# Column norms of the squared weights: adding the row tiles on GpSimd ahead of one product with ones

## The chip, the cores and the metric

The kernel runs on one core of a Trainium2 chip. The metric is the device time of one execution in microseconds (us), the median of several. A core has TensorE (PE in the profile, with PEld for the loading of weights into the array), VectorE (DVE), ScalarE (ACT), GpSimd (POOL) and SyncE (SP, which here only issues DMAs). Each engine works off its own queue in order and waits on semaphores; an instruction that has to wait holds up all that is queued behind it on that engine.

## The reference, cut to what matters

One layer of a hybrid encoder over 4096 tokens of width 1024:

```
h = rmsnorm(x, pre_norm_g)
q, k, v, g_a, u_p, g_p = split(h @ w_in)            # widths 512, 128, 128, 512, 512, 512
a = banded_attention(q, k, v, rel_bias, sink) * silu(g_a)
p = multiscale_pool(u_p, pool_w, pool_scale) * silu(g_p)
x = x + rmsnorm(concat([a, p]) @ w_out, post_norm_g)
```

multiscale_pool takes a centred mean over windows of 2, 4, 8 and 16 tokens minus the token in each of four channel groups, and then a 128x128 linear map per group (pool_w).

The sums of squares that this change is about do not stand in the reference. The kernel multiplies in pairs of float16 numbers that together carry a float32, and for that it scales each weight matrix by a power of two, taken from the largest sum of squares over a column.

## The kernel before

There are two stages. The first, the part up to about 448 us of the profile, projects x onto the gates and the pooled branch (g_p, u_p, g_a), does the pooling, and prepares all weights. The second does q, k, v, the attention and the output. Only the first is touched.

**Weights.** A weight tile is 128 columns of w_in, held as 128 partitions by 1024 numbers: eight row tiles of 128x128 side by side. The pooled gate g_p, the attention gate g_a (GA in the code) and the pooled branch (UU) have four such tiles each; k, v and q have six in all. For UU the tile is first made on TensorE, as the product of a piece of w_in with pool_w (u_prod), and evicted twice by ScalarE, once squared (u_square), once as it is (u_keep).

**Norms.** `norms` runs over the tiles of a group: ScalarE squares a tile into one of two bf16 buffers (w_square, buffer sqt), and `w_norm` forms on TensorE the product of a 128x128 matrix of ones with each of the eight row tiles, added up in one PSUM tile. So every partition holds the sums of squares of the 128 columns. When all tiles of the group are in, `w_scale` on VectorE takes the largest and makes the power of two (lines 582 to 585). From it ScalarE (w_high) and VectorE (w_low) write the float16 pair that the products of the projection read. The groups are "ga" and "gb" (two tiles each, both of the pooled gate, in spite of the name), "a4" (the four tiles of GA), "u4" (the four of UU, from the loop at line 954), and "b1" (the one value tile, in wb_steps). The profile calls their PSUM tiles n2ga, n2gb, n2a, n2u and n2b. The other tiles of w_b and w_out have only a total formed (total_square) and use the same two buffers.

**Order.** The first stage's order is worked out by a planner, the class Steps. Every step is booked with its engine, a length in us, a key (its due time), what it reads and what it writes. `run` goes through the booked time: an engine that comes free takes the ready step with the lowest key, and a step is ready 0.2 us (GAP) after the last one that it depends on has ended. Then all steps are issued in the order of their booked starts. That order is fixed in the queues; a step that takes longer on the chip than booked makes the queue wait, not change. A squaring is booked with 0.2 + 1024 x 0.00088 = 1.1 us, w_norm with 0.5.

**Around the change.** While a4 is done, TensorE works on `plain` for the pooled gate (products "plain" in the profile, L689), VectorE on the operands of x (b_low, narrow subtractions into xb) and on sums of weights for later row blocks (sum_weights, wide additions into wq, then into raw), through the helper `tt` (L307). GpSimd's work in this stage is the root of the row norms (`root`, lines 323 and 324) and later the gate of the pooling (`pool_gate`, line 885). The products of GA follow those of the pooled gate, and those of UU follow them.

Of the kernel before, what the change touches and what calls it, by code (L numbers as in the profile page):

```python
# [8 lines left out]
F32 = mybir.dt.float32  # L9
# [4 lines left out]
ALU = mybir.AluOpType  # L14
# [3 lines left out]
P = 128  # L18
# [116 lines left out]
def hybrid_layer(ctx: ExitStack, tc, io, out):  # L135
    nc = tc.nc
# [12 lines left out]
    ones16 = const.tile([P, P], BF16, name="ones16")  # L149
# [36 lines left out]
    def scale_pow(dst, n2, floor, top):  # L186

        m2 = comm.tile([P, 1], F32, name="m2", tag="m2")
        nc.vector.tensor_reduce(out=m2, in_=n2, axis=mybir.AxisListType.XY, op=ALU.max)
        scale_of(dst, m2, floor, top)  # L190
# [20 lines left out]
    with ExitStack() as actx:  # L211
        pa = actx.enter_context(tc.tile_pool(name="pa", bufs=1))
        psa = actx.enter_context(tc.tile_pool(name="psa", bufs=1, space=PSUM))
# [14 lines left out]
        sqt = [pa.tile([P, D], BF16, name=f"sq{i}") for i in range(2)]  # L228
# [6 lines left out]
        def turn(name):  # L235
            turns[name] += 1
            return turns[name] % 2
# [44 lines left out]
        do = st.add  # L282
# [4 lines left out]
        def act(n):  # L287
            return 0.2 + n * 0.00088
# [5 lines left out]
        def ld(key, dst, src, mb, r=(), w=()):  # L294
            do("SP", 0.45, key, nc.sync.dma_start, dst, src, r=r, w=w, dma=mb / 0.3)

        def t_scalar(eng, out, in0, s1, op0, s2=None, op1=None):
            if op1 is None:
                eng.tensor_scalar(out=out, in0=in0, scalar1=s1, scalar2=None, op0=op0)
            else:  # L300
                eng.tensor_scalar(out=out, in0=in0, scalar1=s1, scalar2=s2, op0=op0, op1=op1)

        V, G, A = nc.vector, nc.gpsimd, nc.scalar


        def tt(eng, out, in0, in1, op):
            eng.tensor_tensor(out=out, in0=in0, in1=in1, op=op)  # L307
# [211 lines left out]
        for c in range(HK):  # L519
            do("ACT", act(512), -5 + 0.1 * c, first_square, c,  # L520
               r=[f"n0.{c}.0"], w=[f"xsq{c}"])
# [10 lines left out]
        for u in range(2):  # L532
# [3 lines left out]
            for c in range(HK):  # L536
                do("DVE", 0.85, k + 0.5 * c, norm_half, c, u,
                   r=["gs"] + [f"bc{i}" for i in (2 * u, 2 * u + 1)],
                   w=[f"n0.{c}.{u}"])
                do("ACT", act(512), k + 0.5 * c + 0.1, b_high, 0, c, u, r=[f"n0.{c}.{u}"],  # L540
                   w=[f"xb0.{c}.{u}h"])
                e, us = ("POOL", 1.4) if c in LOW0[u] else ("DVE", dve(512))
                do(e, us, k + 0.5 * c + 0.2, b_low, 0, c, u,
                   r=[f"n0.{c}.{u}", f"xb0.{c}.{u}h"], w=[f"xb0.{c}.{u}l"])
# [20 lines left out]
        n2_t = {}  # L565
# [7 lines left out]
        def w_norm(z, group, i, n, b):  # L573
            if i == 0:
                n2_t[group] = psa.tile([P, n, P], F32, name=f"n2{group}", tag=f"n2{b}")
            for k in range(KT):
# [2 lines left out]
                    stop=(k == KT - 1), skip_group_check=True,  # L579
                )  # L580

        def w_scale(group, cols):
            scale_pow(sw[:, cols], n2_t.pop(group), 1e-20, W_SCALE)
            t_scalar(V, sc[:, cols], sw[:, cols], gh, ALU.mult)
            V.reciprocal(isc[:, cols], sc[:, cols])
# [4 lines left out]
        def norms(keys, last, views, reads, group, cols):  # L590
            n, b = len(views), turn("n2")
            for i, (key, view, r) in enumerate(zip(keys, views, reads)):
                z = turn("sq")
                do("ACT", act(D), key, w_square, view, z, r=r, w=[f"sqt{z}"])
                do("PE", 0.5, key + 0.5, w_norm, z, group, i, n, b,
                   r=["ones", f"sqt{z}"] + ["summed"] * (group == "ga"), w=[f"n2{b}"])
            do("DVE", 1.5, last, w_scale, group, cols, r=["gs"], w=[f"n2{b}", f"sw{group}"])

        def tile_view(q, i):
# [26 lines left out]
        def sum_weights(q, scale, group, key, step, eng, again=False):  # L626
# [8 lines left out]
            if again:  # L635
# [11 lines left out]
            pair(q, S4, 1, scale, key + 3.5 * step, group)  # L647

        norms([5, 5], 5, [tile_view(GP, i) for i in (0, 1)], [tile_keys(GP, i) for i in (0, 1)],
              "ga", slice(0, 2))  # L650
        do("PE", 1.4, 6, turn_over, 24, r=["ones", "swga"], w=["bankv"])
        do("PE", 0.9, 5.6, row_prod, r=["row", "yt0", "summed"], w=["n20"])
        do("ACT", 0.7, 5.6, row_keep, w=["n20", "yt0"])
        for i, op, key in ((0, A11, 9.5), (1, A12, 12.5)):
            pair(GP, op, i, sw[:, 0:1], key, "ga")
        norms([13, 13], 13, [tile_view(GP, i) for i in (2, 3)], [tile_keys(GP, i) + ["w4h"] * (i == 3) for i in (2, 3)],
              "gb", slice(2, 4))

# [255 lines left out]
        for u in range(2):  # L914
            do("SP", 0.45, 60 + u, lambda u=u: nc.sync.dma_start(x_scr[u], xb[0][:, u]),
               r=[f"xb0.{c}.{h}{v}" for c in range(HK) for h in range(2) for v in "hl"], dma=3.5)


        norms(range(24, 28), 28, [tile_view(GA, i) for i in range(4)],
              [tile_keys(GA, i) for i in range(4)], "a4", slice(4, 8))  # L920

# [31 lines left out]
        U0 = 36.0  # L953
        b = turn("n2")
        for j in range(4):
            ld(9.5 + 0.1 * j, wut[:, j], io["w_uT"][j], 0.5, w=[f"wut{j}"])
            z = turn("sq")
            for half in range(2):
                t = U0 + 4 * j + 2 * half
                do("PE", 1.0, t, u_prod, j, half, r=["ws", f"wut{j}"], w=[f"wup{half}"] + bcs)  # L960
                do("ACT", act(512), t + 1.2, u_square, j, half, z, r=[f"wup{half}"], w=[f"sqt{z}"])
                do("ACT", act(512), t + 1.2, u_keep, j, half, r=[f"wup{half}"],
                   w=[f"tile{UU}.{j}{half}"])
            do("PE", 0.5, U0 + 4 * j + 5, w_norm, z, "u4", j, 4, b, r=["ones", f"sqt{z}"],
               w=[f"n2{b}"])
        for j in range(4):
            do("DVE", 0.01, U0, lambda: None, r=[f"tile{UU}.{j}{half}" for half in range(2)],
               w=[f"tile{UU}.{j}"])
        do("DVE", 1.5, U0 + 18, w_scale, "u4", slice(8, 12), r=["gs"], w=[f"n2{b}", "swu4", "u4"])

        plain_weights(UU, (sw[:, 8:9],) * 2, ("u4",) * 2, (52, 54, 60, 62))
# [868 lines left out]
    V, G = nc.vector, nc.gpsimd  # L1840
# [24 lines left out]
    z = 0.0  # L1865
# [149 lines left out]
    z = now[0]  # L2015
# [177 lines left out]
```

## Time and profile before

| | us |
|---|---|
| time, median of 3 runs | 1161.74 (1161.5 to 1162.57) |
| profiled execution, its own time | 1162.76 |
| profiled execution, span from first to last instruction | 1161.0 |
| VectorE busy in the span | 947.8 (82%) |
| GpSimd busy in the span | 313.7 (27%) |
| mean granted TensorE clock | 0.996 |

How to read it: a row of the timeline gives the start in us, the duration in us, the engine, the line of the kernel, the operation, what it writes and reads, the shape and how many alike were merged; in square brackets stands how long the engine had been idle and who ended that. A row of the table by stretch gives the stretch, its length, and then the busy time and the instructions of PE, PEld, DVE, ACT and POOL, the granted TensorE clock, the share of the DMA engines and GB/s. A row by tile gives the shortest, middle and longest duration in ns, and the first and the last start. Products are pipelined: a record is longer than the time for which it holds the array, and the distance from start to start is what counts.

### The profile page before, as it was taken

What the parts mean: (1) busy time and instruction counts of PE and PEld (TensorE: products, weight loads), DVE (VectorE), ACT (ScalarE), POOL (GpSimd) and SP (SyncE); (2) the same over time, 40 slices, a digit from 0 to 9 for tenths busy, and PEclk for the clock granted to TensorE, in tenths of its full rate; (3) what the DMA queues carried; (4) which work ended last, traced back from release to release, by engine and by line L of the source; (5) the groups of instructions that cost most, each with busy time, mean ns of one, the idle gap of its engine ahead of it and who ended that gap; (6) DMA issues with size and microseconds to landing.
All of it is one profiled execution on the core that took longest, in us unless ns stands there. A gap on an engine that the chain in (4) does not pass through costs nothing. (4 is left out here: it accounts for less than half of the span.)

```text
span 1161.0 us, 32325 instructions
## 1 busy us (share of the span) xinstructions
PE 1146.3 (99%) x13420; PEld 873.5 (75%) x13420; DVE 947.8 (82%) x1875; ACT 717.7 (62%) x1485; POOL 313.7 (27%) x310
## 2 busy tenths in 40 slices
PE   8999999999999999999999999999999999999997
PEld 7998888888888888886667676576666767667653
DVE  6889988988799974568878888878887888887886
ACT  6876556536654542257676776676667677667772
POOL 0001120211111010201524433532533443353231
PEclk8999999999999999999999999999999999999999
DMA  9645575867667664299975886788777688777885
GB/s 344 217 128 180 174 259 183 285 229 238 227 190 225 206 179 134 76 289 242 250 185 144 197 211 143 200 202 177 177 196 184 148 198 215 140 196 165 178 216 143
DMA packets 301683, 228.36 MB, mean 197 GB/s; under 512 B 219568, under 2 KB 259504, under 8 KB 296928
## 3 DMA queue, kind: packets, MB, share of 16 engines
q1 hardware_dynamic: 301536, 226.30, 72.5%
q8 instruction: 105, 1.72, 0.6%
q14 instruction: 42, 0.34, 0.1%
HBM read 114.68 MB, written 60.34 MB: 151 GB/s over the span
## 5 line engine op out<-in xcount | busy, mean ns | idle before, releaser
L689 PEld LDWEIGHTS <-wq 128*128 128x128 f16 x4104 | 401.6, 98 | 50.4 <-DVE wq L310 2.6
L689 PE MATMUL y<-xt,wq 128*128 128x256 f16 x1512 | 203.3, 273 | 0.1
L1347 ACT ACTIVATE p<-p,nm 128x385 f32<-128x385 f32 (+1 forms) x256 | 152.9, 599 | 36.5 <-POOL p L1330 20.3
L1273 PE MATMUL aq<-xb,xb 128*128 128x256 f16 x1024 | 173.4, 273 | 0.2 <-DVE mo L1715 0.2
L1273 PEld LDWEIGHTS <-xb 128*128 128x128 f16 x1536 | 150.1, 98 | 26.4 <-issue 8.0
L1676 PE MATMUL ms<-wo,ys 128*128 128x512 f16 x720 | 163.7, 379 | 0.0
L1377 DVE SCALAR_TENSOR_TENSOR pn<-p,rd,pn 128x384 f16<-128x384 f32 (+1 forms) x256 | 157.6, 667 | 5.9 <-ACT pn L1369 5.9
L1336 DVE CUSTOM_DVE_ANT_0 p<-s,nt,nsink 128x384 f32<-128x384 f32 (+1 forms) x256 | 156.0, 666 | 2.0 <-PE s L1313 2.0
L1273 PE MATMUL aq<-xb,xt 128*128 128x256 f16 x512 | 139.6, 273 | 0.4 <-issue 0.4
L1369 ACT ACTIVATE pn<-p,rd 128x384 f16<-128x384 f32 (+1 forms) x256 | 134.8, 596 | 4.4 <-issue 1.1
L307 POOL TENSOR_TENSOR yt<-yt,sg 128x512 f32<-128x512 f32 (+2 forms) x32 | 51.0, 1594 | 301.6 <-DVE yt L310 214.8
L1676 PEld LDWEIGHTS <-ys 128*128 128x128 f16 x720 | 68.1, 98 | 83.9 <-POOL ys L1582 4.8
L1676 PE MATMUL m<-wo,y 128*128 128x512 f16 x540 | 121.8, 379 | 0.0
L1676 PEld LDWEIGHTS <-y 128*128 128x128 f16 x540 | 51.4, 98 | 63.5 <-ACT at L1543 2.9
L1273 PE MATMUL kv<-xb,xb 128*128 128x256 f16 x512 | 86.7, 273 | 0.0
L1710 POOL TENSOR_TENSOR mo<-mo,gpost 128x512 f32<-128x512 f32 x39 | 63.7, 1634 | 84.4 <-ACT jkb L1699 83.2
L1273 PEld LDWEIGHTS <-xt 128*128 128x128 f16 x768 | 75.1, 98 | 10.6 <-issue 0.8
L689 PE MATMUL plain<-xb,wq 128*128 128x256 f16 x576 | 68.0, 276 | 2.1 <-DVE wq L310 2.0
L1273 PE MATMUL kv<-xb,xt 128*128 128x256 f16 x256 | 69.8, 273 | 0.0
L689 PE MATMUL v<-xt,wq 128*128 128x256 f16 x504 | 68.6, 273 | 0.1
L689 PE MATMUL v<-xb,wq 128*128 128x256 f16 x504 | 68.6, 273 | 0.0
L689 PE MATMUL y<-xb,wq 128*128 128x256 f16 x504 | 68.6, 273 | 0.0
(221 smaller groups left out, 1854.3 us busy)
## 6 DMA issues: line engine op xcount, KB each, us to landing
nt<-in_xT SPq DMA_DIRECT2D x28, 512.0 KB
x_scr<-xb SPq DMA_DIRECT2D x14, 1024.0 KB
xb<-x_scr SPq DMA_DIRECT2D x14, 1024.0 KB
xr<-in_x SPq DMA_DIRECT2D x28, 512.0 KB
out<-xr SPq DMA_DIRECT2D x28, 512.0 KB
xn<-in_x SPq DMA_DIRECT2D x27, 512.0 KB
ga_scr<-cc SPq DMA_DIRECT2D x64, 128.0 KB
raw<-in_w_out SPq DMA_DIRECT2D x16, 512.0 KB
```

The lines of the kernel that those rows point to most:

```text
L307: eng.tensor_tensor(out=out, in0=in0, in1=in1, op=op)
L689: nc.tensor.matmul(b[:, s], wq[:, slot[q, op], wv, s, k, :], x[:, xv, k, :], start=(first and k + s + wv + xv == 0), stop=(last and k == H ...
L1273: nc.tensor.matmul(acc, w[:, j, k, :], x[:, kh, v, kt, :], start=(n == 0), stop=(n == 3 * KT - 1),)
L1336: nc.vector.tensor_tensor_reduce(out=p_t[b, half][:, hh, :nk], in0=s_t[jj][:, gg, :nk], in1=bias[:, h, lo : lo + nk], scale=negc[:, h : h ...
L1347: nc.scalar.activation(p[:, hh, : nk + 1], p[:, hh, : nk + 1], AF.Exp, bias=nm_t[b, half][:, hh : hh + 1], scale=-1.0, accum_out=den_t[b, ...
L1369: nc.scalar.activation(prob_view(b, half)[:, 0, i], p_t[b, half][:, i, :nk], AF.Copy, scale=rd_t[b, half][:, i : i + 1],)
L1377: nc.vector.scalar_tensor_tensor(out=pn4[:, 1, i], in0=p_t[b, half][:, i, :nk], scalar=rd_t[b, half][:, i : i + 1], in1=pn4[:, 0, i], op0= ...
L1676: nc.tensor.matmul(z_t[u, tag], y[:, k, yi, :], wo[o][:, wi, k, :], start=(n == 0 and acc is None), stop=(n == 3 * HK - 1), skip_group_che ...
L1710: eng.tensor_tensor(out=mo, in0=mo, in1=gpost[:, cs], op=ALU.mult)
```

## The change

For the groups a4, u4 and b1, GpSimd adds the squared tile's upper half onto its lower half three times (512, 256 and then 128 columns, in place), and TensorE forms one product of the ones with the 128 columns that are left. The groups ga and gb stay as they were. In the planner the fold is booked on GpSimd with 2.4 us, at the key that w_norm had in `norms`, and the product with 0.1 at a key 2.0 higher. In the loop for u4 the keys are U0 + 4j + 4 for the fold and U0 + 4j + 6 for the product, in place of U0 + 4j + 5.

```diff
+        def w_fold(z):
+            for n in (4, 2, 1):
+                tt(G, sqt[z][:, : n * P], sqt[z][:, : n * P], sqt[z][:, n * P : 2 * n * P], ALU.add)
+
+        def w_norm1(z, group, i, n, b):
+            if i == 0:
+                n2_t[group] = psa.tile([P, n, P], F32, name=f"n2{group}", tag=f"n2{b}")
+            nc.tensor.matmul(
+                n2_t[group][:, i], ones16, sqt[z][:, :P], start=True, stop=True,
+                skip_group_check=True,
+            )
+
+        def w_sums(key, z, group, i, n, b, r):
+            if group in ("ga", "gb"):
+                do("PE", 0.5, key, w_norm, z, group, i, n, b, r=r, w=[f"n2{b}"])
+            else:
+                do("POOL", 2.4, key, w_fold, z, w=[f"sqt{z}"])
+                do("PE", 0.1, key + 2.0, w_norm1, z, group, i, n, b, r=r, w=[f"n2{b}"])
...
-                do("PE", 0.5, key + 0.5, w_norm, z, group, i, n, b,
-                   r=["ones", f"sqt{z}"] + ["summed"] * (group == "ga"), w=[f"n2{b}"])
+                w_sums(key + 0.5, z, group, i, n, b,
+                       ["ones", f"sqt{z}"] + ["summed"] * (group == "ga"))
...
-            do("PE", 0.5, U0 + 4 * j + 5, w_norm, z, "u4", j, 4, b, r=["ones", f"sqt{z}"],
-               w=[f"n2{b}"])
+            w_sums(U0 + 4 * j + 4, z, "u4", j, 4, b, ["ones", f"sqt{z}"])
```

## The prediction

> **What bounds the kernel now.** I read the busy shares of the page first, then the table of busy time by stretch for the stage that the change touches, then the waits of TensorE, and last the timeline.
>
> ```profile
> PE 1146.3 (99%) x13420; PEld 873.5 (75%) x13420; DVE 947.8 (82%) x1875; ACT 717.7 (62%) x1485; POOL 313.7 (27%) x310
> ```
> ```profile
> 28.00:32.00 4.00, 4.00 (x43) 3.64 (x41) 4.00 (x10) 2.48 (x4) 0.00 (x0) 1.00 1.07 349
> 32.00:36.00 4.00, 4.00 (x48) 3.68 (x45) 4.00 (x6) 3.47 (x5) 0.00 (x0) 1.00 1.04 434
> ...
> 44.00:48.00 4.00, 4.00 (x39) 3.67 (x38) 1.80 (x3) 3.50 (x7) 0.00 (x0) 1.00 0.33 134
> ...
> sum 48.00, PE 48.00 PEld 44.23 DVE 39.11 ACT 39.98 POOL 2.44; mean PE 4.00 PEld 3.69 DVE 3.26 ACT 3.33 POOL 0.20
> ```
> ```profile
> PE x L689 <- DVE ubuf L310: 0.5, 1, 0.5
> ```
>
> The columns of the table are PE, PEld, DVE, ACT, POOL. TensorE works without a hole from 28 to 76 us, VectorE is full from 28 to 36, and GpSimd does 2.44 us in all. Between 25 and 160 us TensorE waited 0.5 us for anybody. So TensorE sets the time here: what it no longer does is won in full, and a wait put into its queue is lost in full, because nothing later leaves room to catch up (99% of the whole span).
>
> **What the change removes.** The rows of the squared tiles show how many products there are, and the timeline how long they hold the array.
>
> ```profile
> L577 PE MATMUL n2a<-sq,ones x32: 219/219/219, 31.5 to 37.1; 128*128 128x128 bf16 x32
> L577 PE MATMUL n2u<-sq,ones x32: 219/219/219, 48.4 to 64.7; 128*128 128x128 bf16 x32
> ...
> L577 PE MATMUL n2b<-sq,ones x8: 219/219/219, 151.8 to 152.2; 128*128 128x128 bf16 x8
> ```
> ```profile
> 30.05 1.05 ACT L568 ACTIVATE sq<-raw 128x1024 bf16<-128x1024 f32 x1
> 30.97 0.69 DVE L307 TENSOR_TENSOR xb<-xb,xb 128x512 f16<-128x512 f32 x1
> ...
> 31.45 0.61 PE L577 MATMUL n2a<-sq,ones 128*128 128x128 bf16 x8
> 31.57 1.22 DVE L307 TENSOR_TENSOR wq<-wq 128x1024 f32<-128x1024 f32 x1
> ...
> 31.90 2.13 PE L689 MATMUL plain<-xb,wq 128*128 128x256 f16 x18
> 32.04 2.00 ACT L568 ACTIVATE sq<-raw 128x1024 bf16<-128x1024 f32 x2
> 32.71 1.29 DVE L307 TENSOR_TENSOR xb<-xb,xb 128x512 f16<-128x512 f32 x2
> ...
> 33.91 1.22 DVE L307 TENSOR_TENSOR wq<-wq 128x1024 f32<-128x1024 f32 x1
> ...
> 35.17 1.23 DVE L307 TENSOR_TENSOR wq<-wq 128x1024 f32<-128x1024 f32 x1
> ```
>
> Nine tiles are touched (four of n2a, four of n2u, one of n2b; ga and gb keep the old form). Eight products begin at 31.45 and the next work at 31.90, so one costs 0.45/8 = 0.056 us of TensorE, not the 219 ns of its record, which is latency. Of 72 products 9 remain: 63 x 0.056 = **3.5 us less**.
>
> **What it adds.** Each of the nine tiles gets three additions on GpSimd, 512, 256 and 128 columns wide, in place, and a wait of TensorE for the last.
>
> ```profile
> 22.63 0.23 POOL L299 TENSOR_SCALAR ssq<-ssq 128x2 f32<-128x2 f32 x1 [11.15 <-ACT nt L319]
> ```
> ```profile
> 103.18 1.25 POOL L307 TENSOR_TENSOR yt<-yt,sg 128x504 f32<-128x504 f32 x1 [2.32 <-DVE yt L310]
> ...
> 116.23 1.26 POOL L307 TENSOR_TENSOR yt<-yt,sg 128x504 f32<-128x504 f32 x1 [11.80 <-DVE yt L310]
> ```
>
> No bf16 addition of GpSimd stands in the trace. From 0.23 us for next to no columns and 1.25 for 504 I estimate 1.27, 0.75 and 0.49 us: 2.5 a tile. The ends are 1.27 + 0.63 + 0.32 = 2.2 (proportional to width) and 3 x 1.27 = 3.8 (width free). The plan that orders the queues books 2.4 for the fold, so alone the fold is about as long as booked. The single product is booked at 0.1.
>
> But GpSimd does not run alone. Look at what VectorE did beside its multiplications:
>
> ```profile
> 103.62 1.90 DVE L310 SCALAR_TENSOR_TENSOR wq<-wq,sw 128x1024 f16<-128x1024 f32 x1
> ```
> ```profile
> 116.62 1.44 DVE L307 TENSOR_TENSOR yt<-ubuf 128x527 f32<-128x527 f32 x1
> ...
> 118.09 0.71 DVE L307 TENSOR_TENSOR ws<-yt 128x525 f32<-128x525 f32 x1
> ```
> ```profile
> 98.54 1.22 DVE L307 TENSOR_TENSOR xt<-nt,xt 128x1024 f16<-128x1024 f32 x1
> 98.70 2.17 POOL L307 TENSOR_TENSOR yt<-yt,sg 128x504 f32<-128x504 f32 x1 [4.96 <-DVE yt L310]
> ```
> ```profile
> 52.10 5.00 DVE L307 TENSOR_TENSOR raw<-raw 128x1024 f32<-128x1024 f32 x4
> ...
> 55.47 0.47 POOL L299 TENSOR_SCALAR ssq<-ssq 128x4 f32<-128x4 f32 x1 [31.79 <-ACT nt L319]
> 56.02 1.97 POOL L307 TENSOR_TENSOR rs<-ssq,mhalf 128x4 f32<-128x4 f32 x1
> ```
>
> The 527-column addition of VectorE began 0.39 us into GpSimd's 1.26 and took 1.44 where its neighbour takes 0.71: it got its data when GpSimd was through. The other way round, GpSimd's multiplication began 0.16 us into a 1.22 us subtraction and took 2.17 instead of 1.25. So an operation of VectorE with two SBUF operands and one of GpSimd go one after the other. The last rows show who is next: a small operation of GpSimd ended at 55.94, the next stood ready at 56.02, and yet it ended only at 57.99, after the fourth addition of VectorE's run (52.10 + 5.00 = 57.10). VectorE slips in between two operations of GpSimd. The Trainium skill, "SBUF — State Buffer", section "SBUF: two separate sides", says the same of the shared port pair: an exclusive lock held for the whole instruction, with the loser fully blocked. The trace agrees (1.44 against 0.71). The Trainium skill, "GPSIMD Engine Reference", section 4.1, assigns an elementwise addition to VectorE, as about twice as fast; that speaks against the place chosen here, and the price below does not use it.
>
> **The sum for the four tiles of n2a.** Their fold falls into the full stretch. The first square ends at 30.05 + 1.05 = 31.10. With the plan's own lengths (0.2 us from engine to engine, 2.4 a fold, one fold behind the other) the four single products are due at 33.9, 36.3, 38.7 and 41.1. Their due times in the plan (24 to 28 plus 2.5) are ahead of the products that lie ready, so each is put in TensorE's queue just where it is booked, and blocks it when the fold is late; behind it stand products of the plain gate that need nothing from it.
>
> Now with alternation, taking VectorE's operations at their distances from start to start (1.14 us for the wide, 0.60 for the narrow). Fold 0 waits for the narrow subtraction (to 31.6), then 1.27; a wide addition 1.14; 0.75; a narrow one 0.6; 0.49: it ends near 35.9, and the product goes at 36.0, **2.0 us late**. Fold 1 goes on from there: 0.6 + 1.27 + 1.14 + 0.75 + 1.14 + 0.49 = 5.4, to 41.3; due at 36.3 + 2.0, its product goes at 41.4, another **3.1 late**. Then VectorE's supply of wide operations is nearly used up (after 36.3 come short ones), fold 2 ends near 44.0 and its product is due at 43.8: 0.3. Fold 3 is on time. Sum 5.4 us. With one wide operation more between the adds of fold 2 and of fold 3 each it is 7.7; with no exclusion it is 4 x 0.1 = 0.4. With the fold at 2.2 or 3.8, four folds change by -1.2 or +5.2.
>
> What else waits: squares 2 and 3 (counted from 0, as the folds) write the two buffers again, so ScalarE waits for single products 0 and 1, with the silu evictions of the plain gate behind them; VectorE's scale of the group follows the last product. The gate weights are then ready some 9 us later than before (the scale's first row moves from 37.4 to about 46.6). TensorE's list reaches them at 49.76, plus the 3.8 us net by which it has slipped by then (5.4 less four tiles at 0.39): 53.6, and scale and split take 6.2 us in the rows below (from 37.37 to 42.33 + 2.48/2 = 43.57, the first tile's end), so to 52.8. I book nothing, with 0.8 us of cover.
>
> ```profile
> 37.37 0.69 DVE L189 TENSOR_REDUCE m<-n2a 128x1 f32<-128x512 f32 x1
> ```
> ```profile
> 42.33 2.48 DVE L310 SCALAR_TENSOR_TENSOR wq<-raw,sw,wq 128x1024 f16<-128x1024 f32 x2
> ...
> 49.76 1.47 PE L689 MATMUL plain<-xb,wq 128*128 128x256 f16 x12
> ```
>
> **The four tiles of n2u and the one of n2b.** VectorE has gaps here (1.80 busy of 44 to 48), so folds 0, 2 and 3 should run as booked. Fold 1 starts when the squares end at 51.24 and meets the run of four wide additions at 52.10: two of 1.14 and part of a third, some 2.9 us late, of which TensorE's old margin takes 1.4 (square ends 51.24, product at 52.62).
>
> ```profile
> L568 ACT ACTIVATE sq<-raw x5: 1041/1052/1057, 30.0 to 137.1; 128x1024 bf16<-128x1024 f32 x5
> ```
> ```profile
> 50.64 0.60 ACT L943 ACTIVATE sq<-wup 128x512 bf16<-128x512 f32 x1
> ...
> 52.62 0.61 PE L577 MATMUL n2u<-sq,ones 128*128 128x128 bf16 x8
> ...
> 62.74 1.06 PE L443 MATMUL bc<-ident,rs 128*128 128x128 f32 x8
> ```
>
> I book **1.5 us**; the ends are 0 and 2.9. The roots of the next row block (55.47) queue behind that fold on GpSimd; their spread on TensorE comes at 62.74, so they have 4.7 us of cover from 57.99. The n2b tile is due behind products with earlier due times, its square (the last of the five above, from 137.1) ends 13 us ahead of its product at 151.8, and GpSimd is mostly free: nothing. VectorE loses up to 9 x 2.5 = 22 us in waits and has 48.00 - 39.11 = 8.9 idle in the table; TensorE's own lateness covers part of the rest. I take 0 and keep up to 4.
>
> Sum: -3.5 + 5.4 + 1.5 = **+3.4 us**. The profiled execution took 1162.76 us (span 1161.0 and 1.76 around it), 1.0 above the median 1161.74. From the median: 1165.1.
>
> **The rivals.**
> *The gain stays (faster).* If a GpSimd operation keeps VectorE out only for its reads, or the plan, which sorts every queue anew, puts the low-priority additions outside the folds, the waits are at most 0.4 us, and -3.5 + 0.4 = -3.1: 1158.6. It decides at folds of 2.5 us beside a busy VectorE; from 3.3 us on a fold, four of them eat the gain. For it speaks that those wide additions serve only the next row block; against it, that VectorE has idle time only after 44 us. This is the other side of my forecast.
> *Gain and waits cancel (same).* Fold 0 meets only narrow subtractions and fold 1 one wide addition: 1.2 + 0.6 + 1.1 = 2.9, and 0.6 for n2u: 0, so 1161.7.
> *The clock drops and VectorE falls behind (much slower).* In the start, TensorE stood idle for half of two stretches and ran at half clock just after.
>
> ```profile
> 16.00:18.00 2.00, 0.90 (x14) 0.67 (x12) 2.00 (x6) 2.00 (x4) 0.00 (x0) 1.00 1.05 396
> 18.00:20.00 2.00, 1.09 (x8) 0.88 (x9) 2.00 (x4) 2.00 (x3) 0.00 (x0) 0.86 1.06 417
> 20.00:22.00 2.00, 2.00 (x15) 1.66 (x14) 2.00 (x5) 1.43 (x4) 0.00 (x0) 0.50 1.02 416
> ```
>
> Waits of 2.0 and 3.1 us in n2a could do it again: each stretch of half clock, about 3 us here, loses 1.5. With two of them, and 2.5 us for a late VectorE, +3.4 + 3.0 + 2.5 = +8.9: 1170.6. The Trainium skill, "TensorE: Matmul & The Clock Gate", section "HAM oscillation — how this bites in real kernels", warns of idle gaps over some 3.4 us; by that threshold neither wait alone would do it.
>
> **How the numbers follow.** Forecast (1164.0 to 1168.5) 0.50, gain stays 0.17, cancel 0.20, much slower 0.13. What a measurement can tell from no change here is about 0.2%, 2.3 us. Faster 0.17, same 0.20, slower 0.63. The range from 1158.8 to 1170.0 takes in most of the fast rival and leaves out the end of the slow one; about 0.18 lies outside.
>
> **What will show it.** Right: three GpSimd rows per tile, of 1.3 to 2.4, 0.8 to 1.9 and 0.5 to 1.7 us, between VectorE rows that are each 0.5 to 1.3 longer than their twins; TensorE idle ahead of single products of n2a, ended by GpSimd, some 5 us in all. Wrong: folds of 2.2 to 2.6 us and no such idle time (then 1158.6); idle time at the gate's first product, ended by VectorE (then the 0.8 us of cover was too little); a granted clock under 1.00 between 33 and 50.

## The result, and the profile after

| | before | after |
|---|---|---|
| median | 1161.66 us (1161.5 to 1162.57, 4 runs) | 1168.6 us (1167.63 to 1170.44, 4 runs) |
| ratio to before | | 1.006 (1.0043 to 1.0077) |
| profiled execution, span | 1162.76, 1161.0 | 1168.17, 1166.4 |
| mean granted clock in it | 0.996 | 0.995 |

The changed kernel is slower by 6.9 us in the medians and by 5.4 in the two profiled executions. First the page's busy shares, after:

```profile
PE 1143.1 (98%) x13357; PEld 868.7 (74%) x13357; DVE 952.8 (82%) x1875; ACT 718.7 (62%) x1485; POOL 350.3 (30%) x337
```

TensorE has its 63 products fewer (13357 for 13420) and 3.2 us less of busy time. GpSimd has 27 instructions and 36.6 us more. The 27 additions themselves take 32.2 us (16.3 for the nine of 512 columns, 9.0 for those of 256, 6.9 for those of 128); the rest comes from GpSimd's other work, which takes longer. VectorE has 5.0 us more. Now the busy time by stretch of after, for the stage in which a4 is done (columns as before: PE, PEld, DVE, ACT, POOL, granted clock, DMA share, GB/s):

```profile
28.00:32.00 4.00, 4.00 (x39) 3.69 (x37) 4.00 (x9) 2.79 (x5) 1.13 (x1) 1.00 1.09 352
32.00:36.00 4.00, 2.17 (x20) 1.78 (x20) 4.00 (x6) 1.25 (x2) 3.92 (x2) 1.00 0.98 381
36.00:40.00 4.00, 1.92 (x13) 1.47 (x13) 3.90 (x9) 1.63 (x2) 3.76 (x5) 0.84 0.96 388
40.00:44.00 4.00, 4.00 (x29) 3.11 (x28) 2.64 (x3) 2.94 (x4) 3.84 (x4) 0.73 0.47 160
44.00:48.00 4.00, 3.79 (x36) 3.30 (x34) 1.85 (x3) 2.60 (x6) 3.28 (x4) 1.00 0.54 157
```

Where TensorE was busy without a hole before, it now works for 2.17 and 1.92 of two times 4 us, and behind that its clock is 0.84 and 0.73. VectorE, at 4.00, is as full as it was. The waits of after between 20 and 165 us say who ended the idle time (total, times, longest):

```profile
PE n2a L589 <- POOL sq L307: 4.1, 2, 3.9
PE n2u L589 <- POOL sq L307: 1.7, 3, 0.8
PE plain L708 <- DVE wq L310: 0.8, 1, 0.8
ACT sq L568 <- PE n2a L589: 5.8, 2, 5.1
```

Nearly all of n2a's wait is one wait, for fold 0. These are the rows of the timeline around it, of TensorE, of GpSimd and of VectorE, each in a fence of its own:

```profile
32.04 2.13 PE L708 MATMUL plain<-xb,wq 128*128 128x256 f16 x18
38.08 0.22 PE L589 MATMUL n2a<-sq,ones 128*128 128x128 bf16 x1 [3.92 <-POOL sq L307]
38.14 3.46 PE L708 MATMUL plain<-xb,wq 128*128 128x256 f16 x18
```
```profile
30.87 4.97 POOL L307 TENSOR_TENSOR sq<-sq 128x512 bf16<-128x512 bf16 x1 [7.14 <-ACT sq L568]
35.92 1.60 POOL L307 TENSOR_TENSOR sq<-sq 128x256 bf16<-128x256 bf16 x1
```
```profile
30.67 0.68 DVE L307 TENSOR_TENSOR xb<-xb,xb 128x512 f16<-128x512 f32 x1
31.27 1.22 DVE L307 TENSOR_TENSOR wq<-wq 128x1024 f32<-128x1024 f32 x1
32.40 1.29 DVE L307 TENSOR_TENSOR xb<-xb,xb 128x512 f16<-128x512 f32 x2
33.61 1.22 DVE L307 TENSOR_TENSOR wq<-wq 128x1024 f32<-128x1024 f32 x1
34.74 1.12 DVE L299 TENSOR_SCALAR cg<-isc 128x4 f32<-128x4 f32 x1
```

The first addition starts at 30.87 while VectorE is in a subtraction that ends at 31.35. With alternation it would have its turn there. But VectorE goes on with a wide addition, two narrow subtractions and another wide addition without a break, and only at the end of that one, at about 34.7, does GpSimd get through: the addition ends at 35.84, and an undisturbed one takes 1.15 us (shown below, with old a4). The small operation at 34.74, 128x4, then takes 1.12 us, because now VectorE waits. Fold 0 is through at 38.0, 7.2 us after its start, and TensorE stood idle for 3.92. Eighteen products of the gate take 2.13 us at 32.04 and 3.46 at 38.14: half clock for a part of the second eighteen.

To see where time is won and lost, I set every TensorE product (those with ones left out) beside its twin in before's trace and took the difference of the starts. The table below gives this shift by the time in before, in us. The planner gives each kernel an order of its own, so single products move by a few us against each other. At 120 and 440 the value is therefore only the middle of the products around that time, good to about 1 us (up to 3 in late sums at 120):

```
                products    30      66     120     440    1080    1150   1080 to 1150
after            13357    -0.31   +5.95   +5.95   +5.45   +4.71   +5.39    +0.68
warm             13357    -0.23   +6.84   +6.84   +6.36   +5.76   +5.48    -0.28
old a4           13385    -0.02   +0.01   +0.01   -0.72   -0.99   +1.32    +2.31
no fold          13357    -0.02   -3.15   -2.57   -3.31   -4.04   -4.01    +0.03
booked 4         13357    +0.06   +8.05   +9.64   +9.43   +9.47   +9.34    -0.13
late sums        13357    +1.16   +3.78  +10.00   +8.34   +7.83   +7.55    -0.28
only a4          13392    +0.42   +5.66   +6.42   +6.63   +6.20  +10.11    +3.91
vector           13357    -0.05   -2.85   -0.01   -1.07   -1.63   -2.00    -0.37
old, late sums   13420    +0.07   +0.12   +0.12   +2.04   +1.43   +1.88    +0.45
vector u4        13385    -0.23   -1.79   -1.79   -1.22   -2.03   +2.38    +4.41
half             13384    -0.34   -2.40   -0.19   -0.64   -1.44   +0.91    +2.35
split            13357    -0.09   +7.88   +7.88   +7.39   +6.62   +7.42    +0.80
count            13420    +0.83   -0.73   -0.73   -0.14   -0.24   -0.22    +0.02
```

In after everything is lost between 34 and 66 us; from there to the end it is within 1.3. The other rows are those of the experiments.

### The profile page after: what moved, and what is told of

It is laid out like the page before. It is cut to its first block, busy times and chain, and to the rows that moved or that the text cites. A ratio compares the mean times of both kernels' runs of the same rounds, so it can differ in the third digit from the quotient of the medians.

```text
span 1166.4 us, 32221 instructions
## 1 busy us (share of the span) xinstructions
PE 1143.1 (98%) x13357; PEld 868.7 (74%) x13357; DVE 952.8 (82%) x1875; ACT 718.7 (62%) x1485; POOL 350.3 (30%) x337
## 5 line engine op out<-in xcount | busy, mean ns | idle before, releaser
L1600 POOL TENSOR_TENSOR ys<-at,ys 128x512 f16<-128x512 f32 x29 | 38.9, 1340 | 102.0 <-ACT ys L1596 102.0
```

The source lines that it names most:

```text
L1600: eng.tensor_tensor(out=y[:, :, 1], in0=f(u), in1=y[:, :, 0], op=ALU.subtract)
```

## The experiments

Each is a short edit of the changed kernel (one, "old, late sums", of the kernel before). The kernel before ran beside them: median 1161.93 us (11 runs) beside the first ones, 1162.46 beside the two with late sums, only a4 and vector (21 runs), 1162.27 beside vector u4, half and split (21 runs) and 1162.22 beside count (15 runs). Each ratio is to the runs beside the kernel. The theory was: GpSimd's additions and VectorE's operations exclude each other, and the folds of a4 lie where VectorE is full, so TensorE waits for them. The first rival was that GpSimd's first addition of this kind is dear in itself.

**An addition on GpSimd at the start (warm).**

```diff
+        def first_add16():
+            G.memset(sqt[0][:, : 2 * P], 0.0)
+            tt(G, sqt[0][:, :P], sqt[0][:, :P], sqt[0][:, P : 2 * P], ALU.add)
+
+        do("POOL", 0.6, -9, first_add16, w=["sqt0"])
```

> One small bf16 addition on GpSimd is put at the start, where GpSimd idles; all else is the changed kernel. Theory A (GpSimd had to wait until VectorE's unbroken run of two-operand instructions, 30.67 to 34.82 us, came to its end): the first addition of the first fold stays at about 4.97 us and TensorE's wait for the first single product at about 3.9 us; time as the changed kernel, 1168. Theory B (the first addition of this kind on GpSimd costs some 3.8 us once, whatever VectorE does): the first addition of fold 0 takes 1.2 to 2.3 us, the wait falls from 3.9 to about 1 us, no stretch of half clock follows it, and the time falls by 3 to 5 us, to about 1164. The Trainium skill, GPSIMD Engine Reference, section 2.1, speaks for B: it gives about 6 us for the first call of a freshly loaded kernel.

Measured: 1167.41 us (1166.96 to 1168.38, 5 runs), ratio 1.0047 (1.0033 to 1.0061). GpSimd's timeline of this kernel has the first addition of a4 unchanged, at 4.97 us:

```profile
30.95 4.97 POOL L307 TENSOR_TENSOR sq<-sq 128x512 bf16<-128x512 bf16 x1 [7.14 <-ACT sq L573]
```

The rival falls, and the time is that of the first theory. The Trainium skill, "GPSIMD Engine Reference", section 2.1, speaks of a first call that costs about 6 us; no run here shows one for these additions: the one at the start took 0.42 us for 128 columns.

**a4 as it was, only u4 and b1 folded (old a4), and the reverse (only a4).**

```diff
-            if group in ("ga", "gb"):
+            if group in ("ga", "gb", "a4"):
```
```diff
-            if group in ("ga", "gb"):
+            if group != "a4":
```

> The four tiles of a4 keep their eight products each; only u4 and b1 are folded. If the loss sits in a4 (waits 4.1 us and a stretch of half clock), the time is that of before less 5 x 0.39 = 2.0 us plus the waits for n2u (1.7 us in the changed kernel's profile): 1161 to 1162. If the first addition of its kind costs 3.8 us once, it now falls on the first fold of u4, whose product had 1 to 2 us of margin: 1162 to 1164. If a4 is not the cause: 1167 and more.

> Only the four tiles of a4 are folded; u4 and b1 keep eight products a tile. If a4 carries the loss: before, less 4 x 0.39, plus the wait of 4.1 us, a stretch of half clock of 1.7 and the gate weights' 0.8: +5.0, 1166.9. If u4 carries it: 1163 or less. With the run in which only u4 and b1 were folded at +3.5, the two should add up to the changed kernel's +6.9 if the parts are independent, which would put this one at +3.4, 1165.3.

Measured: 1165.43 us (1164.04 to 1167.4, 6 runs), 1.0031 (1.0019 to 1.0042), for old a4; 1171.35 (1170.2 to 1175.18, 5 runs), 1.0083 (1.0068 to 1.0098), for only a4. As times both miss (1161 to 1162 and 1166.9 were expected). In the first stage they do tell the parts apart: by 66 us the shift is +0.01 without a4's folds and +5.66 with them alone, together the +5.95 of after within 0.3. So the loss up to there is a4's, and the folds of u4 give back what their products save. The very first fold of old a4, in GpSimd's timeline, took no more than any undisturbed one, which speaks against the first rival once more:

```profile
45.72 1.15 POOL L307 TENSOR_TENSOR sq<-sq 128x512 bf16<-128x512 bf16 x1 [21.89 <-ACT sq L962]
```

What spoils the two times lies at the other end, after 1080: +2.3 and +3.9 in the last column of the table, where after has +0.7. That comes up again below.

**No additions at all (no fold).** The single product is formed from the first row tile alone; seven of eight row tiles are left out of the norms.

```diff
-                do("POOL", 2.4, key, w_fold, z, w=[f"sqt{z}"])
-                do("PE", 0.1, key + 2.0, w_norm1, z, group, i, n, b, r=r, w=[f"n2{b}"])
+                do("PE", 0.1, key, w_norm1, z, group, i, n, b, r=r, w=[f"n2{b}"])
```

> The additions on GpSimd are left out, and the nine single products take the first row tile alone, so the norms leave out seven of eight row tiles. This measures the gain by itself: 63 products less at 0.056 us, -3.5 us, 1158.2. Rival: the products filled holes of TensorE, or what follows is late anyway; then -2 us or less, 1159.7 and more.

Measured: 1158.52 us (1157.98 to 1158.81, 6 runs), 0.9969 (0.9958 to 0.9981). That is 3.4 below before: the gain by itself is as large as worked out, and the additions cost about 10 us (1168.6 less 1158.5).

**The wide sums of VectorE held back (late sums), and the same in the kernel before.** VectorE's wide additions for the pooled gate wait until a4's scale is made, so that the folds of a4 meet narrow operations only.

```diff
-                do(eng, us, k, tt, e, o, x, y, op, r=quarter_keys(q, xi) + quarter_keys(q, yi),
+                do(eng, us, k, tt, e, o, x, y, op,
+                   r=quarter_keys(q, xi) + quarter_keys(q, yi) + ["swa4"] * (q == GP),
```

> The changed kernel, but VectorE's wide additions of the pooled gate's weights (needed only from about 94 us on) wait for the scale of a4, so that they can't lie beside the folds of a4. Theory A (the fold is late because VectorE's two-operand instructions keep GpSimd out): fold 0 falls from 7.2 us to 2.4 to 4, the wait for n2a from 4.1 us to 1 or less, no half clock follows, and the time falls by 4 to 6 us, to 1163 to 1165, less if VectorE's late additions cost something later. Theory C (something else than VectorE delays the first addition by 3.8 us): it still takes about 5 us, and the wait stays near 3.9.

> The kernel before with the same later additions as in the late-sums run, as its control. If VectorE has room for them later: as before, 1161.5 to 1162.5. If it has not: TensorE waits for VectorE between 75 and 125 us, and the time rises by 1 to 4 us, which is then to be taken off the late-sums run.

Measured: 1170.87 us (1169.58 to 1172.01, 5 runs), 1.0072 (1.0059 to 1.0085), with the folds; 1164.18 (1162.44 to 1165.24, 11 runs), 1.0014 (1.0006 to 1.0023), without. First GpSimd's timeline with the folds, then TensorE's waits of that kernel between 20 and 165, then its clock by stretch:

```profile
32.34 1.49 POOL L307 TENSOR_TENSOR sq<-sq 128x512 bf16<-128x512 bf16 x1 [8.62 <-ACT sq L568]
```
```profile
PE n2u L589 <- POOL sq L307: 4.9, 3, 2.4
PE x L709 <- DVE ubuf L310: 3.7, 1, 3.7
PE n2a L589 <- POOL sq L307: 0.5, 3, 0.2
```
```profile
36.00:40.00 4.00, 3.81 (x37) 3.28 (x35) 3.67 (x7) 3.63 (x5) 3.77 (x5) 1.00 0.91 287
40.00:44.00 4.00, 3.82 (x37) 3.27 (x35) 0.52 (x1) 2.15 (x5) 2.94 (x5) 1.00 0.93 251
```

For a4 the theory holds: with the wide additions gone, the same fold 0 has its first addition in 1.49 us for 4.97, TensorE waits 0.5 us in n2a for 4.1, and between 36 and 44 us there is no half clock. But the wide additions are needed: put off, they meet the folds of u4 (4.9 us for 1.7), and VectorE comes late to the pooling (3.7 us at one product; behind that the granted clock is 0.61 from 124 to 128). As a time late sums misses (1163 to 1165 were expected). Without folds the same delay costs 1.7 us (1164.18 less 1162.46). With these taken off, late sums still lies 6.7 us above before, about as far as after does: the loss moved from a4 to later products and did not shrink. VectorE's work can be moved, but hardly put anywhere for nothing.

**A fold booked longer (booked 4).** The planner books 4.0 us for a fold, near to what a4's four took on average in after (16.57 us from the start of the first to the end of the last, 4.1 each).

```diff
-                do("POOL", 2.4, key, w_fold, z, w=[f"sqt{z}"])
+                do("POOL", 4.0, key, w_fold, z, w=[f"sqt{z}"])
```

> The planner books a fold with 4.0 us in place of 2.4, nothing else. If the loss is TensorE standing in front of a single product that was put into its queue too early, the waits for n2a and n2u go from 5.8 us to under 2, and the later weights cost something instead: 1161 to 1166. If the fold's length itself is the loss (the weights come too late whatever is booked): 1168 and more.

Measured: 1171.14 us (1170.7 to 1176.08, 5 runs), 1.0088 (1.0072 to 1.0103): not the 1161 to 1166 of the first reading, but the 1168 and more of the second. The waits of TensorE between 20 and 165 in this kernel, and from its timeline and its stretches the wait for fold 0 and what followed:

```profile
PE n2a L589 <- POOL sq L307: 2.6, 1, 2.6
PE plain L708 <- DVE wq L310: 2.0, 1, 2.0
PE wup L957 <- ACT sq L962: 1.7, 2, 1.3
```
```profile
38.45 0.22 PE L589 MATMUL n2a<-sq,ones 128*128 128x128 bf16 x1 [2.61 <-POOL sq L307]
```
```profile
40.00:44.00 4.00, 4.00 (x25) 2.95 (x24) 4.00 (x5) 2.93 (x5) 3.84 (x4) 0.62 0.63 203
...
52.00:56.00 4.00, 2.28 (x10) 1.61 (x10) 3.79 (x11) 4.00 (x6) 1.06 (x2) 0.66 0.01 2
56.00:60.00 4.00, 2.60 (x13) 1.86 (x14) 4.00 (x5) 4.00 (x7) 0.00 (x0) 0.50 0.23 47
```

Booked longer, the single products stand further back in TensorE's queue, the wait for fold 0 is 1.3 us shorter, and n2u is not waited for at all. But the norms are done later too, and with them the gate's weights: most of what n2a saves stands again at the first product that reads them (2.0 for 0.8). And the clock fell to half twice: for 3.4 us after the wait of 2.61 us, and from 53.3 on for twice as long, which by half clock alone is 1.7 and 3.4 us lost.

**All additions on VectorE (vector).**

```diff
-                tt(G, sqt[z][:, : n * P], sqt[z][:, : n * P], sqt[z][:, n * P : 2 * n * P], ALU.add)
+                tt(V, sqt[z][:, : n * P], sqt[z][:, : n * P], sqt[z][:, n * P : 2 * n * P], ALU.add)
...
-                do("POOL", 2.4, key, w_fold, z, w=[f"sqt{z}"])
+                do("DVE", 1.2, key, w_fold, z, w=[f"sqt{z}"])
```

> The folds run on VectorE instead of GpSimd, booked with 1.2 us. VectorE then has no partner to wait for, and a fold is one engine's work in turn. If the loss comes from GpSimd and VectorE excluding each other: the waits for n2a and n2u fall to under 1 us together, and the time comes near the run without folds (1158.5), at 1158.5 to 1161, as far as VectorE has room for nine times about 1 us. If any fold in front of the product costs more than it saves: 1162 and more.

Measured: 1161.64 us (1160.77 to 1164.6, 11 runs), 0.9998 (0.9989 to 1.0007): the time of before, above the 1158.5 to 1161 that were expected. The tile's row for VectorE, and TensorE's waits between 20 and 165:

```profile
L307 DVE TENSOR_TENSOR sq<-sq x27: 224/292/426, 31.5 to 156.9; 128x512 bf16<-128x512 bf16 x9, 128x256 bf16<-128x256 bf16 x9, 128x128 bf16<-128x128 bf16 x9
```
```profile
PE v L708 <- DVE cc L307: 1.5, 1, 1.5
PE y L708 <- DVE xb L307: 1.0, 1, 1.0
```

A fold takes some 1.0 us there, no product of the norms waits, and by 66 us the shift is -2.85. The nine folds are 9 us of VectorE, though, and at about 105 to 120 us, where it prepares the operands of the pooling, it is late by 2.8 (good to about 1, as the table is there). From 440 on the kernel is 1.1 to 2.0 ahead in its profile; its median is no better than before.

**Less work for VectorE: only u4 and b1 (vector u4), or one halving a tile (half).** The first takes the VectorE version and leaves a4 out as in old a4. The second makes one addition of 512 columns a tile, on VectorE, and four products; they are booked with 0.5 and 0.25.

```diff
-            for n in (4, 2, 1):
-                tt(G, sqt[z][:, : n * P], sqt[z][:, : n * P], sqt[z][:, n * P : 2 * n * P], ALU.add)
+            for n in (4,):
+                tt(V, sqt[z][:, : n * P], sqt[z][:, : n * P], sqt[z][:, n * P : 2 * n * P], ALU.add)
...
-            nc.tensor.matmul(
-                n2_t[group][:, i], ones16, sqt[z][:, :P], start=True, stop=True,
-                skip_group_check=True,
-            )
+            for k in range(4):
+                nc.tensor.matmul(
+                    n2_t[group][:, i], ones16, sqt[z][:, k * P : (k + 1) * P], start=(k == 0),
+                    stop=(k == 3), skip_group_check=True,
+                )
```

> u4 and b1 are folded on VectorE (booked 1.2 us), a4 keeps its eight products. Gain of the products: 5 tiles x 7 x 0.056 = 2.0 us. Theory 'the additions cost only where they meet a full VectorE': u4's folds fall between 44 and 66, where VectorE has idle time, so no wait for n2u and most of the gain stays: 1160.5 us (1159.5 to 1161.5), a shift near -2 at 66 and at 440. Rival 'whatever VectorE is given there comes back as lateness at 90 to 130', as with all nine tiles on VectorE: shift -2 at 66, near 0 from 130 on, and 1162.0 to 1163. Rival 'the end of the kernel decides', with longer waits for the transposing DMA after 1060: 1164 or more.

> VectorE adds only the upper half of a squared tile to the lower one (one addition of 512 columns, 0.42 us, booked 0.5), for all nine tiles, and TensorE forms four products. Gain: 9 x 4 x 0.056 = 2.0 us, for 9 x 0.42 = 3.8 us of VectorE. Theory 'VectorE's lateness goes with the work that it is given': three full additions a tile (9 us) gave back about 1.9 of 3.4, so this gives back 0.8: 1161.2 us (1160.3 to 1162). Rival 'nothing comes back': shift -2.0 all along, 1160.4. Rival 'everything does': 1162.4.

Measured: 1165.49 us (1162.91 to 1167.23, 11 runs), 1.0023 (1.0014 to 1.0032), and 1165.96 (1162.82 to 1168.17, 11 runs), 1.0026 (1.0017 to 1.0034). Up to 1080 the first theory holds for vector u4: -1.8 at 66, -1.2 at 440, -2.0 at 1080, no wait in u4. For half, the lateness at 120 is 2.2 us where 0.8 was expected, though that value is good to about 1 only. Both times miss, and what was ahead is lost at the end, as vector u4's last rival has it. TensorE's waits after 1040, first of vector u4, then of half:

```profile
PE o L1501 <- DMA pt<-pn: 3.6, 2, 2.4
```
```profile
PE o L1502 <- DMA pt<-pn: 3.0, 2, 1.8
```

TensorE waits there for a DMA that transposes the attention weights, in a stage that no edit touches. In vector u4 the longer of its two waits is followed by a granted clock of 0.72 from 1108 to 1112, and in only a4 (3.0 us of the same wait) by 0.68 from 1116 to 1120; half and old a4 (3.0 each) have no half clock there. That parts the +4.41 and +3.91 of the table's last column from the +2.35 and +2.31.

**The number of products (count).** The four kernels that lose at the end have 13384 to 13392 products, all others 13357 or 13420. This kernel is vector u4 with 35 more idle products at the start, in a gap.

```diff
-        do("PE", 5.5, -9, turn_over, 52, r=["ones"], w=["bankv", "turned"])
+        do("PE", 5.5, -9, turn_over, 87, r=["ones"], w=["bankv", "turned"])
```

> The version with u4 and b1 folded on VectorE once more, with 35 more of the first idle products (52 to 87), which fill the 1.87 us that TensorE waits ahead of its first product of the gain (35 x 0.056 = 2.0). It asks about the end of the second stage: after 1040, TensorE waited 0 to 1.5 us in all for the transposing DMA in the nine kernels with 13420 or 13357 products, and 3.0 to 3.6 in the four with 13384 to 13392. With the 35 this kernel has 13420 products again, and all else is as it was. Theory 'the end goes by how many instructions stand in TensorE's queue ahead of it': wait at most 1.5 us, shift about -1.5 to -2 at the end as at 66 to 1080, 1160.3 us (1159.3 to 1161.5). Rival 'it goes by something else' (the time at which the stage is reached, the order on another queue): wait again 3 us or more, 1164.5 to 1166. If the idle products delay the start, the shift at 30 shows it and is taken off.

Measured: 1162.2 us (1160.89 to 1164.45, 11 runs), 0.9999 (0.999 to 1.0008), beside 1162.22 of before. The page's busy shares of this kernel, and all of TensorE's waits after 1040:

```profile
PE 1144.1 (99%) x13420; PEld 871.3 (75%) x13420; DVE 950.8 (82%) x1890; ACT 718.3 (62%) x1485; POOL 314.8 (27%) x310
```
```profile
PE z L1666 <- DVE xb L1733: 0.6, 1, 0.6
PE s L1331 <- DVE nm L1354: 0.2, 1, 0.2
```

The wait for the transposing DMA is gone, and the last column of the table is +0.02 for +4.41. The predicted gain on before did not come: the start is 1.06 us later than in vector u4 (half clock between 20 and 24), and 0.6 more is lost by 440, as in vector u4. So the longer wait at the end goes with the number of products in all 14 traces, and went away in the one test in which that number was put back. That test is not clean, since the 35 products also moved the start and its clock. The time at which the stage is reached is not what decides: the long wait is there at shifts of -2.03 (vector u4) and +6.20 (only a4) at 1080, and not at -1.63 (vector) and +4.71 (after). Why the number should matter, no run shows; values between these were not tried.

**The first addition cut in two (split).** It asks what made the first addition wait for 3.8 us.

```diff
-            for n in (4, 2, 1):
+            for h in (0, 2):
+                tt(G, sqt[z][:, h * P : h * P + 2 * P], sqt[z][:, h * P : h * P + 2 * P], sqt[z][:, h * P + 4 * P : h * P + 6 * P], ALU.add)
+            for n in (2, 1):
```

> The changed kernel with the first addition of a fold cut into two of 256 columns (0.67 us each undisturbed), all on GpSimd. It asks why the very first addition of a4 took 4.97 us and was passed over at four ends of VectorE's operations. If the length of the waiting operation decides, the first half gets its turn at the next end (within 1.9 us of its start), fold 0 gets one more turn to wait for, and n2a waits about as long in sum but in smaller pieces. If the stretch decides (VectorE's unbroken run from 31.3 to 34.8), the first half is held to about 34.7 again, n2a's first wait is about 4.5 us, and the time is 1169 to 1171.

Measured: 1170.25 us (1169.29 to 1170.64, 4 runs), 1.0068 (1.0054 to 1.0082). The half, in GpSimd's timeline, and VectorE's rows to the point at which it got through:

```profile
31.09 4.49 POOL L307 TENSOR_TENSOR sq<-sq 128x256 bf16<-128x256 bf16 x1 [7.14 <-ACT sq L568]
```
```profile
31.48 1.22 DVE L307 TENSOR_TENSOR wq<-wq 128x1024 f32<-128x1024 f32 x1
32.62 1.28 DVE L307 TENSOR_TENSOR xb<-xb,xb 128x512 f16<-128x512 f32 x2
33.83 1.22 DVE L307 TENSOR_TENSOR wq<-wq 128x1024 f32<-128x1024 f32 x1
34.96 0.64 DVE L299 TENSOR_SCALAR cg<-isc 128x4 f32<-128x4 f32 x1
```

An addition of half the size is held up through the same four operations, and gets through at 35.58 - 0.67 = 34.9. Time and row are as expected if the stretch decides, and not the length of the waiting operation. What is different about this run of VectorE stays open.

## Why the prediction was right, and where it was too low

Forecast were 1165.1 us, in a range of 1158.8 to 1170.0, and slower; 1168.6 is inside the range and 0.1 above the 1164.0 to 1168.5 that had half of the chances. The sign was right, and so was the mechanism in the main: GpSimd and VectorE keep each other out where VectorE is full, and TensorE waits for a4's folds. The size was half of what came: +3.4 against +6.9 in the medians and +5.4 in the profiled pair. Two of the prediction's own signs of being wrong came true besides: a granted clock under 1.00 between 33 and 50, and a wait for VectorE at the gate's first product. Some of its terms came out right in sum but not in their parts. By its steps:

- *The gain, -3.5 for 63 products.* Right: -3.4 without the additions.
- *The length of a fold, 2.5 undisturbed.* Right: 1.15 + 0.67 + 0.43, and 0.08 between them.
- *GpSimd and VectorE exclude each other.* Right: with the wide additions out of the way n2a's wait falls from 4.1 to 0.5. The Trainium skill, "SBUF — State Buffer", section "SBUF: two separate sides", has the same exclusive lock, and the traces agree that one waits for the other (in after 1.60 us for an addition that takes 0.67 undisturbed). The addition of 4.97 us, though, waited through more than one instruction.
- *They alternate, "VectorE slips in between two operations of GpSimd".* This is the step that failed, for one addition: the first of fold 0 was passed over at four ends of VectorE's operations, so that fold 0 ended at 38.0 and not at 35.9. The rest got their turn at the end of VectorE's current operation. Fold 1, which was to take 5.4 us, took 3.4, to 41.39, because by then VectorE was mostly at short operations; its product was not waited for, since TensorE, at half clock, was through with the 18 products ahead of it only at 41.44. In all, n2a's wait was 4.1 us (3.92 for fold 0, 0.21 for fold 3) where 5.4 were booked (2.0, 3.1 and 0.3). That the sum is near is partly luck: one term was too small by 1.9, the next too large by 3.1.
- *The clock.* It was left to the last rival, with a price of 1.5 us for each drop, because two waits of 2.0 and 3.1 were thought likely to stay below what brings it on. One wait of 3.92 came, and with it clocks of 0.84 and 0.73: 4 x 0.16 + 4 x 0.27 = 1.7 us that were not in the sum.
- *The gate's weights: "I book nothing, with 0.8 us of cover".* TensorE waited 0.8 us for them: the cover was gone. The scale's first row came at 47.99, where 46.6 was expected.
- *n2u, 1.5.* The sum is right, 1.7, and without a4's folds the shift at 66 is 0. The reason given is not: fold 1, the only one booked as late, was not waited for, and folds 0, 2 and 3, which should have run as booked, were. These are TensorE's rows of the four products in after's timeline:

```profile
52.64 0.22 PE L589 MATMUL n2u<-sq,ones 128*128 128x128 bf16 x1 [0.24 <-POOL sq L307]
...
61.31 0.22 PE L589 MATMUL n2u<-sq,ones 128*128 128x128 bf16 x1
...
68.06 0.22 PE L589 MATMUL n2u<-sq,ones 128*128 128x128 bf16 x1 [0.70 <-POOL sq L307]
...
71.28 0.22 PE L589 MATMUL n2u<-sq,ones 128*128 128x128 bf16 x1 [0.81 <-POOL sq L307]
```

Folds 2 and 3 began only at 65.59, behind the roots of the next row block, which GpSimd did from 62.36 on. The right sum is luck.

- *n2b, 0, and VectorE's knock-on, 0.* Right for after: the shift falls by 0.5 from 66 to 440. VectorE was thought to lose up to 22 us in waits; its busy time grew by 5.0. It is no rule, as VectorE's lateness at 120 us in late sums and vector shows.

With the measured terms the sum is -3.5 + 4.1 + 1.7 + 0.8 + 1.7 = +4.8, beside +5.4 in the profile. Most of what is missing lies in how a wait is read. The idle time in brackets counts from the end of the last record, and from start to start more is lost: the last of the eighteen products at 32.04 began at 33.89 and the next product at 38.08, 4.19 us later instead of 0.11, so the wait shown with 3.92 cost 4.08. Taken so, the six waits between 30 and 72 us, 6.6 in brackets, cost 7.6. With the clock's 1.7 and eight tiles' gain of 3.1 that makes +6.2, and the table has -0.31 to +5.95 from 30 to 66. Later the shift falls by 1.2 up to 1080 and rises by 0.7 after it. The medians lie 1.5 us further apart than the two profiles do. In after's runs the time goes with the granted clock: 1167.63 at 0.998, 1168.17 at 0.995, 1169.03 at 0.994, 1170.44 at 0.992. So the clock's part differs from run to run; in which stretch the slower runs lost it was not seen.

Of the rivals, "the gain stays" gave 1158.6, which is what the kernel without additions took (1158.5): its condition, waits of at most 0.4 us, was the false one. The last, the clock and a late VectorE, came about in its first half.

## What to carry to other kernels

A saving on the bounding engine counts only as far as what replaces it arrives in time: 63 products were worth 3.4 us, and the additions that stood for them cost about 10 on an engine that was idle for 73% of the span, because they and VectorE's operations kept each other out just where VectorE was full. Look at the stretch in which the moved work falls, not at the engine's mean share, and reckon with a falling clock behind a long wait of the bounding engine: after's one wait of 3.92 us cost 1.7 more. Before a late, untouched stage is blamed or praised for a small difference, see whether the same wait comes and goes with edits that have nothing to do with it, as the transposing DMA's did here.

## What the runs showed of the hardware that was not expected

- An addition of GpSimd that waits for VectorE can be passed over several times: 4.97 us for 1.15 of work, through four operations of VectorE, in every kernel with that run (4.49 for 0.67 in split). Elsewhere it had its turn at the end of the current operation.
- The exclusion also holds up small operations of VectorE with one operand: the 128x4 TENSOR_SCALAR took 1.12 us at 34.74 in after, beside GpSimd's addition. VectorE's timeline of before, where GpSimd is idle, has it undisturbed:

```profile
35.05 0.17 DVE L299 TENSOR_SCALAR cg<-isc 128x4 f32<-128x4 f32 x1
```

- A wait of 2.61 us was followed by a granted clock of 0.62 over the next 4 us (booked 4). The Trainium skill, "TensorE: Matmul & The Clock Gate", section "HAM oscillation — how this bites in real kernels", puts the gap that does this at some 3.4 us; after's 3.92 agrees with it, and this one does not. The length of the wait alone does not decide: at the end of vector u4 half clock followed a wait of 2.4 us, and behind the one of 2.4 in late sums (n2u) there was none.
- With thirty-five idle products more at the start, a wait of 3.6 us for a DMA a thousand microseconds later was gone. It is one test, and the cause is open.
